# Seven products in place of eight for one unit of a weight pair, w_down in rounds, and transposes finished by gather DMAs

## The chip, the cores and the metric

One core of one Trainium2 chip runs the kernel. The metric is the device time of one execution in microseconds (us). It is set by the core's five engines, which run their own instruction queues and wait for each other through semaphores: TensorE (PE; PEld for its weight loads), VectorE (DVE), ScalarE (ACT), GpSimd (POOL) and SyncE (SP), and by 16 DMA engines.

## The reference

Two layers of a decoder trunk, batch 1, 256 positions, width 2048, all in float32. What is computed in one layer:

```python
h = rms_norm(x, mix_norm[l])
proj = h @ w_in[l]                                  # 2048 x 7680
q, k, v, uv, gate_logits = split(proj)              # 1024, 256, 256, 2048, 4096 columns
q, k = rope(rms_norm(q)), rope(rms_norm(k))         # heads of 64
branch_a = sliding_window_attention(q, k, v, sinks) @ w_attn_branch[l]      # 1024 x 2048
branch_b = chunked_sgu(gelu(uv), w_spatial, ...) @ w_sgu_branch[l]          # 1024 x 2048
merged = sigmoid(gates_a) * branch_a + sigmoid(gates_b) * branch_b
x = x + merged @ w_out[l]                           # 2048 x 2048
h2 = rms_norm(x, ffn_norm[l])
x = x + (silu(h2 @ w_gate[l]) * (h2 @ w_up[l])) @ w_down[l]   # 2048 x 5632, twice; 5632 x 2048
```

The weights, 475 MB in all, are read once from HBM.

## The kernel before, in words

**Matmuls.** A float32 product is made of three passes in the type float32r: an operand is split into a rounded part (hi) and a remainder (lo), and `a_hi w_hi + a_hi w_lo + a_lo w_hi` is summed in PSUM (lines 202, 203 and 204). One matmul takes 128 rows of the contraction, 128 positions and 512 columns.

**Chunks, parts and units.** The weights form one list of chunks of 512 columns in the order of use. A chunk is loaded in halves of 256 rows, 512 KB each, on SP's queue (`Stream.load`, L115), into one of 4 buffers `raw`. `Stream.split` makes `hi` (ScalarE, L128) and `lo` (VectorE, L129) of a half, into one of 3 buffers each; such a split half is called a part here. A part feeds 12 matmuls: 2 halves of the positions, 2 blocks of 128 rows, 3 passes. `Stream.next` keeps loads 5 and splits 3 parts ahead of the part that TensorE takes, so far as buffers are free.

The activations are held in units of 512 features, transposed (features on partitions), as `uh` and `ul`. `product(units)` runs over all parts of a chunk and sums into two PSUM banks, one for each half of the positions; four banks in all, so two chunks alternate.

**Transposes.** `transposed` turns an activation of 256 x 512. `turn` does it on VectorE, 16 instructions of 32 x 256 for each unit (L216), in four steps, and the split of the turned unit follows 4 and 5 steps after the call. With `on_pe` the turning is done by 8 TensorE transposes into two PSUM banks instead (L246); this is used for the first norm's four units and for the last unit before a product needs it. `kT` and `qT` of the attention are made by `turn` as well.

**Order.** TensorE's instructions run in the order in which the program is written. The order on the other engines is set by a scheduler that plays the program through. `after(n, fn)` puts a piece of side work (attention, gelu, transposes, norms) n slots later; `tick()` ends a slot, one for each part, and issues what is due behind the last split.

**Stages of a layer.** k/v, two chunks of q, two of v, two of u, four of the first gate, four of `w_attn_branch`, then alternately a second gate chunk and a chunk of `w_sgu_branch`, four of `w_out`, eleven times gate and up, four of `w_down` (each over all 11 hidden units). `residual` adds a finished chunk to `xs`, and prepares the next norm: its unit (2 slots later), its squares and, at the last chunk, its `rstd`.

**Slots of SBUF.** Units, gates, hidden chunks and attention tiles share one pool of 29 slots of 4 KB per partition.

Of the kernel before, what the change touches and what calls it, by code (L numbers as in the profile page):

```python
# [31 lines left out]
W_LOAD = 5  # L32
W_SPLIT = 3
N_WARM = 8
TT = 1
K_TURN = 7
Q_TURN = 7
Q_FIRST = 12
Q_STEP = 5
LOAD_BY = (1, 3, 4, 4)  # L40
# [5 lines left out]
def hybrid_trunk(ctx: ExitStack, tc: tile.TileContext, x, mix_norm, w_in, q_norm, k_norm, sinks,  # L46
# [6 lines left out]
    big = ctx.enter_context(tc.tile_pool(name="big", bufs=29))  # L53
    wraw = ctx.enter_context(tc.tile_pool(name="wraw", bufs=4))
    wsp = ctx.enter_context(tc.tile_pool(name="wsp", bufs=3))
    tmp = ctx.enter_context(tc.tile_pool(name="tmp", bufs=5))
    turned = ctx.enter_context(tc.tile_pool(name="turned", bufs=TT))
    small = ctx.enter_context(tc.tile_pool(name="small", bufs=4))
    ps_acc = ctx.enter_context(tc.tile_pool(name="ps_acc", bufs=4, space=bass.MemoryType.PSUM))
# [19 lines left out]
    def cols_of(w_ap, n):  # L79
        return [w_ap[:, j * CW:(j + 1) * CW] for j in range(n)]  # L80

    O_KV, O_U, O_V, O_GATE = QW, QW + 2 * KVW, QW + 2 * KVW + SW, QW + 2 * KVW + 2 * SW
    NF = FF // CW
    chunks = []
    for l in range(DEPTH):
        wl = w_in[l]
        for o in (O_KV, 0, CW, O_V, O_V + CW, O_U, O_U + CW):
            chunks.append(wl[:, o:o + CW])
        chunks += cols_of(wl[:, O_GATE:O_GATE + D], NCH)
        chunks += cols_of(w_attn_branch[l], NCH)  # L90
        for j in range(NCH):
            chunks.append(wl[:, O_GATE + D + j * CW:O_GATE + D + (j + 1) * CW])
            chunks.append(w_sgu_branch[l, :, j * CW:(j + 1) * CW])
        chunks += cols_of(w_out[l], NCH)
        for f in range(NF):
            chunks.append(w_gate[l, :, f * CW:(f + 1) * CW])
            chunks.append(w_up[l, :, f * CW:(f + 1) * CW])
        chunks += cols_of(w_down[l], NCH)
    halves = [(w, h) for w in chunks for h in range(w.shape[0] // (2 * P))]

    class Stream:


# [5 lines left out]
        def load(self, upto):  # L109
            while len(self.raws) < min(upto, len(halves)):  # L110
                w, h = halves[len(self.raws)]
                raw = wraw.tile([P, 2, CW], F32, tag="raw", name=nm("raw"))
                src = w[2 * h * P:2 * (h + 1) * P, :].rearrange("(k p) n -> p k n", p=P)
                if self.raws:
                    self.loaded = nc.sync.dma_start(raw, src)  # L115
                else:
                    for i in range(2):
                        self.loaded = nc.sync.dma_start(raw[:, i:i + 1], src[:, i:i + 1])
                self.raws.append(raw)

        def split(self, upto):
            while len(self.parts) < min(upto, len(halves)):
                raw = self.raws[len(self.parts)]
# [3 lines left out]
                for i in ([slice(0, 1), slice(1, 2)] if one else [slice(0, 2)]):  # L127
                    nc.scalar.activation(hi[:, i, :], raw[:, i, :], AF.Copy)  # L128
                    self.last = nc.vector.tensor_tensor(out=lo[:, i, :], in0=raw[:, i, :], in1=hi[:, i, :].bitcast(F32),  # L129
                                            op=ALU.subtract)  # L130
                self.parts.append((hi, lo))

        def next(self):
            self.load(self.at + W_LOAD)
            self.split(self.at + W_SPLIT)
            self.at += 1
            return self.parts[self.at - 1]
# [10 lines left out]
    def tick():  # L148
        slot_no[0] += 1
# [39 lines left out]
    def product(units):  # L189

        ps = [ps_acc.tile([P, CW], F32, tag="acc", name=nm("acc")) for _ in range(NT)]
        n = 2 * len(units)
        for h in range(n):
            hi, lo = stream.next()
            uh, ul = units[h // 2]
            for t in range(NT):
                for kk in range(2):
                    k = 2 * (h % 2) + kk
                    a, b = uh[:, k, t * P:(t + 1) * P], ul[:, k, t * P:(t + 1) * P]
                    first = h == 0 and kk == 0  # L200
                    last = h == n - 1 and kk == 1
                    nc.tensor.matmul(ps[t], a, hi[:, kk, :], start=first, stop=False)  # L202
                    nc.tensor.matmul(ps[t], a, lo[:, kk, :], start=False, stop=False)  # L203
                    nc.tensor.matmul(ps[t], b, hi[:, kk, :], start=False, stop=last)  # L204
            if h < n - 1:
                tick()
        return ps

    def turn(dst, src):

        iv = src.rearrange("p t (k j c) -> p t k j c", j=4, c=B)
        ov = dst.rearrange("p k (t i c) -> p t k i c", t=NT, c=B)

        def blocks(j):
            for i in range(4):
                nc.vector.transpose(ov[j * B:(j + 1) * B, :, :, i, :], iv[i * B:(i + 1) * B, :, :, j, :])  # L216

        blocks(0)
        for j in range(1, 4):
            after(j, lambda j=j: blocks(j))  # L220

    def transposed(units, c, src, scale=None, cols=None, on_pe=False):

        uh = slot([P, 4, S], F32R, "uh")
        ul = slot([P, 4, S], F32R, "ul")

        def parts(k0, n, src_t):
            step = n if cols is None else 1
            for k in range(0, n, step):
                g = (scale or 1.0) if cols is None else cols[:, k0 + k:k0 + k + 1]  # L230
                nc.scalar.activation(uh[:, k0 + k:k0 + k + step, :], src_t[:, k:k + step, :], AF.Copy, scale=g)  # L231
            for k in range(0, n, step):
                g = (scale or 1.0) if cols is None else cols[:, k0 + k:k0 + k + 1]
                kk = slice(k0 + k, k0 + k + step)
                nc.vector.scalar_tensor_tensor(  # L235
                    out=ul[:, kk, :].rearrange("p k s -> p (k s)"),
                    in0=src_t[:, k:k + step, :].rearrange("p k s -> p (k s)"), scalar=g,
                    in1=uh[:, kk, :].bitcast(F32).rearrange("p k s -> p (k s)"), op0=ALU.mult, op1=ALU.subtract)

        if on_pe:  # L240
            for b in range(2):
# [5 lines left out]
                parts(2 * b, 2, pt)  # L247
            units[c] = (uh, ul)
# [4 lines left out]
        def done():  # L253
            parts(2, 2, tt[:, 2:4])
            units[c] = (uh, ul)

        turn(tt, src)
        after(4, lambda: parts(0, 2, tt))
        after(5, done)

    class Norm:
# [13 lines left out]
        def unit(self, c, on_pe=False):  # L275
            transposed(self.units, c, xs[:, :, c * CW:(c + 1) * CW], cols=self.cols[:, 4 * c:4 * c + 4],
                       on_pe=on_pe)
# [61 lines left out]
    class Layer:  # L339


        def __init__(self, l):
# [7 lines left out]
            self.lng = lay.tile([P, SW], F32, tag="lng", name=f"lng{l}")  # L350
            self.lnb = lay.tile([P, SW], F32, tag="lnb", name=f"lnb{l}")

        def fetch(self, i, eng):
# [7 lines left out]
            else:  # L361
                dst, row = ((self.lng, sgu_ln_g), (self.lnb, sgu_ln_b))[i - 2]
                eng.dma_start(dst, row[l].unsqueeze(0).to_broadcast([P, SW]))

# [23 lines left out]
        def spatial(self):  # L388
            self.wsT = lay.tile([P, G, P], F32, tag="wsT", name=f"wsT{self.l}")
# [8 lines left out]
    def prepare(l):  # L398
        layer[l] = pl = Layer(l)
        after(6, pl.tables)  # L400
        if l:
            for i in range(4):
                pl.fetch(i, nc.gpsimd)
            after(13, pl.spatial)
            return
# [4 lines left out]
    class Attention:  # L410
# [46 lines left out]
        def keys(self, kv):  # L457
# [4 lines left out]
            after(K_TURN, lambda: turn(self.kT, kd.rearrange("p t n a d -> p t (n a d)")))  # L462

        def queries(self, c, q):
# [3 lines left out]
            after(Q_TURN, lambda: turn(self.qT[c], q))  # L468
            n = Q_FIRST + (4 * Q_STEP - 8) * c
# [4 lines left out]
            after(n + 6, lambda: transposed(self.attT, c, self.att[c]))  # L474
# [121 lines left out]
    def gate(units):  # L596
        ps = product(units)
        dst = slot([P, NT, CW], name="gate")
        for t in range(NT):
            nc.scalar.activation(dst[:, t, :], ps[t], AF.Tanh, scale=norm.rh[t])  # L600
        tick()
        return dst

    def residual(units, cols):

        nxt = Norm(cols) if cols is not None else None
        for j in range(NCH):
            ps = product(units)
            for t in range(NT):
                n = 1 if cols is not None or j < NCH - 1 else 2  # L610
                w = CW // n
                for i in range(n):
                    sl = slice(j * CW + i * w, j * CW + (i + 1) * w)
                    nc.vector.tensor_tensor(out=xs[:, t, sl], in0=ps[t][:, i * w:(i + 1) * w], in1=xs[:, t, sl],
                                            op=ALU.add)
                    if cols is None:
# [112 lines left out]
```

## Time and profile before

| | |
|---|---|
| time, median of 2 runs | 2535.38 us (2535.35 to 2535.41) |
| span of the profiled execution, first to last instruction | 2534.6 us; the runs' times are 0.8 us longer than this span |
| granted TensorE clock | 0.999 |
| TensorE, VectorE, ScalarE, GpSimd busy | 2518.1, 1772.1, 1149.8, 47.9 us |
| read from HBM | 475.27 MB, 188 GB/s over the span |

The profile is of one execution. Its parts are the busy time of each engine, 40 slices of the span, the DMA queues, the chain of work that ended last (followed back from the last instruction to what released it), the costliest groups of instructions, and the DMA issues. A group's row reads: line, engine, operation, out<-in, count | busy us, mean ns of one | idle time of the engine just before them, and what ended it. A row of the waits reads: who waited <- for whom: us in total, times, longest. A row of a stretch reads: from:to, its length, then for each engine its busy time and (xinstructions), the granted clock, the DMA share and GB/s. A row of the timeline reads: start, us, engine, line, operation, xcount. Matmuls are pipelined, so a matmul's busy time is longer than the distance to the next.

### The profile page before, as it was taken

How to read it: one execution, taken by the hardware profiler on the slowest of the kernel's cores; microseconds unless marked ns; L12 is line 12 of the kernel's file. 1: busy time of each engine (PE TensorE's matmuls, PEld its weight loads, DVE VectorE, ACT ScalarE, POOL GpSimd, SP SyncE). 2: the span in 40 equal slices, each digit the busy share in tenths (PEclk: the TensorE clock that was granted, in tenths of full speed). 3: DMA queues.
4: the chain of work that ended last, by engine and by line, in shares of the span. 5: the costliest groups of instructions: out<-in, count | busy, mean ns of one | idle time of the engine just before them, and what ended most of it. 6: DMA issues, size and time to landing. Idle time of an engine off the chain costs nothing.

```text
span 2534.6 us, 30238 instructions
## 1 busy us (share of the span) xinstructions
PE 2518.1 (99%) x11306; PEld 2079.3 (82%) x11306; DVE 1772.1 (70%) x2467; ACT 1149.8 (45%) x1386; POOL 47.9 (2%) x51
## 2 busy tenths in 40 slices
PE   9999999999999999999999999999999999999999
PEld 7788888888888888888887888888888888888887
DVE  7987767786766767665679976677767676765444
ACT  5455444454444444444444544444544444444333
POOL 1100000000000000000001000000000000000000
PEclk9999999999999999999999999999999999999999
DMA  7555666566666666666665556666666666666665
GB/s 237 175 170 147 189 198 192 191 202 196 188 195 192 193 197 191 194 195 192 193 183 165 160 151 197 191 192 197 192 191 192 197 189 196 191 198 191 203 204 158
DMA packets 248643, 479.35 MB, mean 189 GB/s; under 512 B 14960, under 2 KB 16592, under 8 KB 248496
## 3 DMA queue, kind: packets, MB, share of 16 engines
q1 hardware_dynamic: 247376, 475.33, 63.0%
q0 software_dynamic: 800, 1.83, 0.4%
q8 instruction: 88, 1.44, 0.3%
q14 instruction: 59, 0.48, 0.1%
q10 hardware_dynamic: 320, 0.27, 0.0%
HBM read 475.27 MB, written 2.10 MB: 188 GB/s over the span
## 4 chain that ended last, share of the span: by engine, by line
PE 94%; DVE 4%; issue 1%; POOL 1%; DMA 0%; ACT 0%; SPq 0%; DVEq 0%; ACTq 0%
PE acc L202 31%; PE acc L203 30%; PE acc L204 30%; DVE wlo L129 1%; DVE qT L216 1%; PE po L523 1%; POOL rq L187 1%; PE ppt L513 0%; PE psc L485 0%; DMA raw<-in_w_in_dram 0%; PE psg L587 0%; DVE kT L216 0%; PE pt L246 0%; DVE sq L441 0%; DVE q L452 0%
## 5 line engine op out<-in xcount | busy, mean ns | idle before, releaser
L129 DVE TENSOR_TENSOR wlo<-raw,whi 128x1024 fp32r<-128x1024 f32 (+1 forms) x898 | 1096.8, 1222 | 704.8 <-ACT whi L128 698.9
L128 ACT ACTIVATE whi<-raw 128x1024 fp32r<-128x1024 f32 (+1 forms) x898 | 949.3, 1058 | 1227.8 <-PE acc L204 1158.4
L203 PE MATMUL acc<-wlo,uh 128*128 128x512 f32 x3584 | 1396.8, 390 | 7.8 <-DVE wlo L129 7.7
L202 PE MATMUL acc<-whi,uh 128*128 128x512 f32 x3584 | 1400.0, 391 | 1.1 <-ACT uh L231 1.1
L204 PE MATMUL acc<-whi,ul 128*128 128x512 f32 x3584 | 1395.6, 389 | 0.0
L203 PEld LDWEIGHTS acc<-wlo,uh 128*128 128x128 f32 x3584 | 673.2, 188 | 151.6 <-DVE wlo L129 13.3
L202 PEld LDWEIGHTS acc<-whi,uh 128*128 128x128 f32 x3584 | 673.3, 188 | 140.7 <-ACT uh L231 1.9
L204 PEld LDWEIGHTS acc<-whi,ul 128*128 128x128 f32 x3584 | 673.1, 188 | 140.5 <-DVE ul L235 0.5
L216 DVE STREAM_TRANSPOSE tt<-hid 32x256 f32<-32x256 f32 x352 | 153.4, 436 | 5.7
L231 ACT ACTIVATE uh<-tt 128x512 fp32r<-128x512 f32 x72 | 41.5, 624 | 53.0 <-DVE tt L216 53.0
L216 DVE STREAM_TRANSPOSE tt<-xs 32x256 f32<-32x256 f32 x144 | 62.8, 436 | 2.3
L235 DVE SCALAR_TENSOR_TENSOR ul<-tt,uh 128x512 fp32r<-128x512 f32 x72 | 49.1, 684 | 0.0
L216 DVE STREAM_TRANSPOSE tt<-gate 32x256 f32<-32x256 f32 x96 | 41.8, 436 | 1.6
L682 ACT ACTIVATE hid<-acc,rhalf 128x512 f32<-128x512 f32 x44 | 30.4, 690 | 21.3 <-PE acc L204 21.3
L683 DVE SCALAR_TENSOR_TENSOR hid<-hid,acc 128x512 f32<-128x512 f32 x44 | 30.1, 684 | 11.6 <-ACT hid L682 11.6
L687 DVE SCALAR_TENSOR_TENSOR hid<-acc,rr,hid 128x512 f32<-128x512 f32 x44 | 30.9, 743 | 0.0
L501 ACT ACTIVATE pr<-pr,negm 128x128 f32<-128x128 f32 (+1 forms) x64 | 28.3, 443 | 5.4 <-DVE negm L494 5.3
L216 DVE STREAM_TRANSPOSE tt<-att 32x256 f32<-32x256 f32 x64 | 27.9, 436 | 1.1
L216 DVE STREAM_TRANSPOSE tt<-u 32x256 f32<-32x256 f32 x64 | 27.9, 436 | 1.0
L216 DVE STREAM_TRANSPOSE qT<-q 32x256 f32<-32x256 f32 x64 | 27.9, 436 | 0.9
L600 ACT ACTIVATE gate<-acc,rhalf 128x512 f32<-128x512 f32 x32 | 22.0, 689 | 13.5 <-PE acc L204 13.5
L187 POOL TENSOR_TENSOR rstd<-var,neg_half 128x1 f32<-128x1 f32 x8 | 5.2, 662 | 1142.5 <-DVE var L284 1142.4
(110 smaller groups left out, 573.3 us busy)
## 6 DMA issues: line engine op xcount, KB each, us to landing
raw<-in_w_in_dram SPq DMA_DIRECT2D x239, 512.0 KB, 4.0
raw<-in_w_gate_dram SPq DMA_DIRECT2D x176, 512.0 KB, 3.8
raw<-in_w_up_dram SPq DMA_DIRECT2D x176, 512.0 KB, 3.9
raw<-in_w_down_dram SPq DMA_DIRECT2D x176, 512.0 KB, 4.2
raw<-in_w_out_dram SPq DMA_DIRECT2D x64, 512.0 KB, 3.8
raw<-in_w_attn_branch_dram SPq DMA_DIRECT2D x32, 512.0 KB, 4.2
raw<-in_w_sgu_branch_dram SPq DMA_DIRECT2D x32, 512.0 KB, 4.1
xs<-in_x_dram SPq DMA_DIRECT2D x8, 256.0 KB, 7.7
```

What stands on the lines that cost most here:

```text
L128: nc.scalar.activation(hi[:, i, :], raw[:, i, :], AF.Copy)
L129: self.last = nc.vector.tensor_tensor(out=lo[:, i, :], in0=raw[:, i, :], in1=hi[:, i, :].bitcast(F32), op=ALU.subtract)
L187: nc.gpsimd.tensor_tensor(out=dst, in0=src, in1=neg_half[:, :n], op=ALU.pow)
L202: nc.tensor.matmul(ps[t], a, hi[:, kk, :], start=first, stop=False)
L203: nc.tensor.matmul(ps[t], a, lo[:, kk, :], start=False, stop=False)
L204: nc.tensor.matmul(ps[t], b, hi[:, kk, :], start=False, stop=last)
L216: nc.vector.transpose(ov[j * B:(j + 1) * B, :, :, i, :], iv[i * B:(i + 1) * B, :, :, j, :])
L231: nc.scalar.activation(uh[:, k0 + k:k0 + k + step, :], src_t[:, k:k + step, :], AF.Copy, scale=g)
L235: nc.vector.scalar_tensor_tensor(out=ul[:, kk, :].rearrange("p k s -> p (k s)"), in0=src_t[:, k:k + step, :].rearrange("p k s -> p (k s)") ...
L682: nc.scalar.activation(th, ps[t], AF.Tanh, scale=norm.rh[t])
L683: nc.vector.scalar_tensor_tensor(out=th, in0=th, scalar=1.0, in1=ps[t], op0=ALU.add, op1=ALU.mult)
L687: nc.vector.scalar_tensor_tensor(out=a[:, t, :], in0=ps[t], scalar=norm.rr[t], in1=a[:, t, :], op0=ALU.mult, op1=ALU.mult)
```

## The change

- **Pairs and loads.** Chunks are taken in pairs of 1024 columns (k/v alone stays 512 wide; the last gate and up chunk form one pair). A load is 1 MB: 256 rows of a pair. Four `raw` buffers of this size, five split buffers (3 before). The parts stay 256 rows x 512 columns.
- **`run(units, done)`** takes the place of `product`. A pair sums into all four accumulator banks; `done(c, ps)` reads column half c as soon as it is finished.
- **Seven products.** For one unit of each pair in `w_out`, gate/up and `w_down` (`M_OUT`, `M_FFN`, `M_DOWN` = 1) the block of 256 positions x 512 rows x 1024 columns is cut into 2 x 2 x 2 and computed by Strassen's method in the form that needs 4 differences of weights, 4 sums of activations and 7 block products. `Stream.split` makes the differences in place in `raw` on VectorE; `combined` makes the sums for the unit. Between the products ScalarE copies four times out of PSUM (two of these copies go to another bank) and VectorE adds twice into a bank. A slot of side work is two such products long.
- **w_down in rounds.** The hidden chunks come in rounds of 4, 4 and 3; after each the residual of this round is added to `xs`.
- **Transposes.** `gathered` takes the place of `turn`: two VectorE instructions transpose the 32 x 32 blocks of a unit in place, and 16 DMAs on GpSimd's queue, 32 KB each, bring the blocks to their places. The reader follows `G_WAIT` = 8 slots after. The turning on TensorE is used for more units: the last two of each residual, of the merged and of each round's hidden units, and one of the attention's.
- **Others.** 23 slots of 4 KB in place of 29; the SGU's scale, shift and `wsT` lie in slots; scores start at slot 19 (12 before).

The core of the diff:

```diff
-W_LOAD = 5
-W_SPLIT = 3
+W_LOAD = 4
+W_SPLIT = 5
+ROUNDS = ((0, 1, 2, 3), (4, 5, 6, 7), (8, 9, 10))
+M_OUT, M_FFN, M_DOWN = 1, 1, 1
...
+    PRODUCTS = ("11", "t1", "t2", "22", "t3", "21", "t4")
...
+                src, total = {"11": ("11", None), "22": ("22", None), "21": ("21", None),
+                              "t1": ("11", ("12", "11")), "t2": ("11", ("22", "11")),
+                              "t3": ("12", ("22", "12")), "t4": ("11", ("21", "11"))}[name]
...
+                raw = self.raws[i][j]
+                if total is not None:
+                    (ia, ja), (ib, jb) = total
+                    nc.vector.tensor_tensor(out=raw, in0=self.raws[ia][ja], in1=self.raws[ib][jb], op=ALU.subtract)
...
+        own = [acc(b) for b in (banks if job.pair else banks[:2])]
+        if job.m:
+            a, e, x, y = own
+            ps = [[x, y], [e, a]]
+            banks[:] = [banks[2], banks[3], banks[1], banks[0]]
+            into = {"11": a, "t1": e, "t2": a, "22": e, "t3": a, "21": x, "t4": y}
...
+            if name != "whole":
+                p = into[name]
+                for k in range(2):
+                    ah, al = unit.block(name, k)
+                    three(p, ah, al, hi[:, k, :], lo[:, k, :], id(p) not in begun, at and k == 1)
+                    begun.add(id(p))
+                if at:
+                    with tc.high_priority():
+                        if name == "11":
+                            nc.scalar.activation(x, a, AF.Copy)
+                        elif name == "t1":
+                            kept("p5", e)
+                        elif name == "t2":
+                            kept("u2", a)
+                        elif name == "22":
+                            nc.vector.tensor_tensor(out=e, in0=e, in1=held["u2"], op=ALU.add)
+                        elif name == "t3":
+                            nc.scalar.activation(y, a, AF.Copy)
+                            nc.vector.tensor_tensor(out=a, in0=a, in1=held["p5"], op=ALU.add)
+                if n < len(job.steps) - 1:
+                    tick(0.5)
+                continue
...
+    def gathered(dst, src):
+
+        blk = turned.tile([P, 4, 4, NT, B], F32, tag="blk", name=nm("blk"))
+        for t in range(NT):
+            nc.vector.transpose(blk[:, :, :, t, :].rearrange("p j k c -> p k j c"),
+                                src[:, t, :].rearrange("p (k j c) -> p k j c", j=4, c=B))
+        ov = dst.rearrange("p k (t i c) -> p i (k t) c", t=NT, c=B)
+        for i in range(4):
+            for j in range(4):
+                nc.gpsimd.dma_start(ov[j * B:(j + 1) * B, i],
+                                    blk[i * B:(i + 1) * B, j].rearrange("p k t c -> p (k t) c"))
...
+        def combined(f):
+            s4 = slot([P, 4, 2, P], name="sums")
+            a11, a12, a21, a22 = (f[:, 2 * h:2 * h + 2, t * P:(t + 1) * P] for t in range(2) for h in range(2))
+            for i, (p, q, op) in enumerate(((a21, a22, ALU.add), (s4[:, 0], a11, ALU.subtract),
+                                            (a11, a21, ALU.subtract), (a12, s4[:, 1], ALU.subtract))):
+                nc.vector.tensor_tensor(out=s4[:, i], in0=p, in1=q, op=op)
+            two(unit.hi, unit.lo, f)
+            two(unit.shi, unit.slo, s4)
+            units[c] = unit
...
+        gathered(tt, src)
+        after(G_WAIT, done)
...
+                if nxt is not None:
+                    after(2, lambda: nxt.unit(o, on_pe=j == 2, sums=sums and o == 0))
...
+                after(2, lambda: transposed(hT, f, a, on_pe=f in fs[-2:], sums=f in fs[:M_DOWN]))
```

More of the change, by code (lines that the diff above doesn't have):

```diff
@@ L196, in product @@
             for t in range(NT):
+                p = ps[c][t]
                 for kk in range(2):
[L198 to L220, printed above, removed]
@@ L240, in transposed @@
         if on_pe:
+            f = turned.tile([P, 4, S], F32, tag="tt", name=nm("tt")) if sums else None
             for b in range(2):
```

441 lines of the change are left out of this document (281 added, 160 removed).

## The prediction

> **What bounds the kernel now.** I read the shares of the engines and the chain first, then the groups of instructions that write or read the accumulators, then a stretch of TensorE's timeline for the pitch, then the waits.
>
> ```profile
> span 2534.6 us, 30238 instructions
> PE 2518.1 (99%) x11306; PEld 2079.3 (82%) x11306; DVE 1772.1 (70%) x2467; ACT 1149.8 (45%) x1386; POOL 47.9 (2%) x51
> q1 hardware_dynamic: 247376, 475.33, 63.0%
> PE 94%; DVE 4%; issue 1%; POOL 1%; DMA 0%; ACT 0%; SPq 0%; DVEq 0%; ACTq 0%
> 0.00:2535.00 2535.00, 2457.17 (x10752) 2014.94 (x10752) 123.27 (x182) 63.32 (x92) 1.00 0.64 189
> ```
>
> The last row is the stretch of the whole run for instructions on the accumulators (busy time of PE, PEld, DVE, ACT): 10752 of TensorE's 11306 matmuls are products with a weight. TensorE carries 94% of the chain; VectorE has 30% free and the DMA queue a third. A matmul's busy time overlaps its neighbours', so its price is the pitch:
>
> ```profile
> 899.65 0.39 PE L202 MATMUL acc<-whi,uh 128*128 128x512 f32 x1
> ...
> 909.85 0.39 PE L202 MATMUL acc<-whi,uh 128*128 128x512 f32 x1
> ```
>
> 45 matmuls lie between these starts: 10.20 / 45 = 0.2267 us. 10752 of them make 2437 us of the span of 2534.6; head, tail, attention and waits share the other 97. So time is gained by issuing fewer matmuls, and lost by letting TensorE wait. It hardly waits now:
>
> ```profile
> SPq L115 <- DVE wlo L129: 1967.7, 843, 6.8
> ACT whi L128 <- PE acc L204: 1158.4, 708, 3.4
> DVE wlo L129 <- ACT whi L128: 698.9, 602, 3.1
> PEld acc L203 <- DVE wlo L129: 13.3, 14, 1.9
> PE acc L203 <- DVE wlo L129: 7.7, 12, 1.5
> ACT whi L128 <- DMA raw<-in_w_in_dram: 3.4, 2, 2.8
> ```
>
> Loads wait for the split, the split for TensorE; only 7.7 us go the other way. Weights are not short, and bigger loads buy nothing by themselves.
>
> **Part 1: the matmuls that go.** A unit (512 rows of the contraction, 1024 columns of a pair) costs 4 parts x 12 = 48 matmuls; by seven products of 2 x 3 = 6 it costs 42. One unit per pair is done so: 2 pairs in w_out, 4 + 4 + 3 in gate/up, 2 x 3 in w_down, 19 per layer, 38 in all. 38 x 6 = 228 matmuls x 0.2267 = **51.7 us** off TensorE. The operands keep tile shape and type, so I keep the pitch.
>
> **Part 2: the transposes that come to TensorE.** Units turned there rise from 9 (72 transposes) to 28: merged 4, attention 2, norms 4 at the start, 4 + 2 at the residuals, hidden 12. One such unit stands in the trace:
>
> ```profile
> 1814.38 0.39 PE L204 MATMUL acc<-whi,ul 128*128 128x512 f32 x1
> 1814.62 1.04 PE L246 MATMUL pt<-ident,xs 128*128 128x128 f32 x8
> 1815.41 0.48 PE L202 MATMUL acc<-whi,uh 128*128 128x512 f32 x1
> 1815.72 0.40 PE L203 MATMUL acc<-wlo,uh 128*128 128x512 f32 x1
> ...
> 1815.83 1.55 ACT L231 ACTIVATE uh<-pt,vcols 128x256 fp32r<-128x256 f32 x4
> ...
> 1817.10 1.65 DVE L235 SCALAR_TENSOR_TENSOR ul<-pt,vcols,uh 128x256 fp32r<-128x256 f32 x4
> ```
>
> From 1814.38 to 1815.72 is 1.34 us where two pitches take 0.45: 0.89 a unit, 19 x 0.89 = **+16.9**. Nine times two such units follow within 2.7 us on the same two PSUM buffers, and the second waits until both engines have read the first. Nothing in the trace shows that pair. Its cost lies between 0 and the 2.92 us (1815.83 to 1818.75) for which a unit is read; since the second comes up to 2.7 us later, I take 0.5 each, near the lower end: **+4** (0 to 26).
>
> **Part 3: what the seven products ask of VectorE and ScalarE.** The rows:
>
> ```profile
> L129 DVE TENSOR_TENSOR wlo<-raw,whi 128x1024 fp32r<-128x1024 f32 x894 | 1094.2, 1224 | 702.1 <-ACT whi L128 696.3
> L128 ACT ACTIVATE whi<-raw 128x1024 fp32r<-128x1024 f32 x894 | 946.8, 1060 | 1227.2 <-PE acc L204 1158.4 <-ACT whi L128 26.4 <-issue 25.9
> L614 DVE TENSOR_TENSOR xs<-acc,xs 128x512 f32<-128x512 f32 x30 | 19.2, 682 | 0.0
> L614 DVE TENSOR_TENSOR xs<-acc,xs 128x256 f32<-128x256 f32 x4 | 1.5, 419 | 5.1 <-PE acc L204 5.1
> L600 ACT ACTIVATE gate<-acc,rhalf 128x512 f32<-128x512 f32 x32 | 22.0, 689 | 13.5 <-PE acc L204 13.5
> 0.00:2535.00 2535.00, 355.61 (x816) 1.00 0.64 189
> ```
>
> (The last is the whole run for the transposes of L216.) Per unit: 7 splits in place of 4 and 4 differences of weights at 1.22, so +8.5 us on VectorE, and +3.2 on ScalarE; 2 sums at 0.68 on VectorE and 4 copies at 0.69 on ScalarE. Over 38 units that is +377 on VectorE and +226 on ScalarE. Three rounds of w_down bring 32 more residual sums (+22), ten units with sums about 2.8 each (four sums of 256 elements at 0.42, 1.22 for one more split, less 0.1), +28. The transposes fall from 356 us to 64 x 0.68 = 44 (estimate from the 512-element row). VectorE 1772 + 377 + 22 + 28 - 312 = **1887 us**, about three quarters of the span: as a mean it fits beside TensorE and costs nothing. In the stretch of seven products it may not. TensorE needs 42 x 0.2267 = 9.5 us for them. Five split buffers mean that four parts are ready when the first product starts; VectorE still owes, within those 9.5 us, 2.44 (t3), 1.22 (21), 2.44 (t4), 1.22 (the first whole part), 1.36 (two sums) and 1.36 (the previous pair's output): 10.04, so 0.5 too much; nothing, if one difference was taken early. Above lies a chain in which VectorE, at one of the differences, idles through ScalarE's 1.06 because the next step needs it: 0.5 + 1.06, about 1.6. I take 0.3, nearest to the sum of rows: 38 x 0.3 = **+11** (0 to 61). A copy out of PSUM adds a wait on TensorE (product t2 writes the bank that ScalarE copies, t3 and t4 likewise), with one product, 1.36 us, to cover 0.17 of drain and 0.69 of copy. What is queued behind on ScalarE are splits of 1.06; one of them ahead of the copy costs 0.5, counted in the upper end.
>
> **Part 4: transposes by gather DMAs.** 32 groups of 16 issues on GpSimd's queue, 32 KB each in runs of 128 B. The nearest rows are two loads of the same size and the same runs:
>
> ```profile
> 1.60 0.89 POOL L313 DMA_DIRECT2D cs<-in_cosine_dram  x1
> 2.50 0.73 POOL L314 DMA_DIRECT2D sn<-in_sine_dram  x1
> 3.22 0.54 POOL L319 DMA_DIRECT2D vrows<-in_mix_norm_dram  x1
> cs<-in_cosine_dram POOLq DMA_DIRECT2D x1, 32.0 KB, 4.5
> sn<-in_sine_dram POOLq DMA_DIRECT2D x1, 32.0 KB, 5.2
> ```
>
> Issues follow each other at 0.73 to 0.89 without waiting for a landing. Sixteen at 0.75 are 12 us, the last lands 4.5 later: 16.5. The reader stands 8 slots of 2.72 us (a part of 12 matmuls) behind: 21.8. So one gather is covered. The added wait stands on ScalarE, with later parts' splits behind it, and TensorE's four parts, 10.9 us, behind those. The block and target tiles have one buffer each: of two units gathered in a row, the second's issues wait until the first is read (about 26 us after the first began), so it is ready at 26 + 16.5 + 3 = 46. On GpSimd's queue the norms' powers stand behind at most 12 us of issues: q and k are issued 7 slots (19 us) after their pair, the next powers come with the next pair, 43.5 us on. Merged, hidden and attention units have over 60 us. The residual's have not: after w_out the next pair (42.2 us) and the Strassen unit (9.5) cover it; after layer 0's w_down the last round's pair is 31.3 and the next unit is wanted 5.4 + 1.8 later, at 38.5: TensorE waits **+7** there (0 if issues run at 0.54; 15 if at 0.89 and late).
>
> The Trainium skill speaks against this: "DMA: Bandwidth & Descriptors", Anatomy of one DMA, fits a GpSimd DMA as 2.0 us plus bytes over 436 GB/s, by which 16 in a row would be 33 us, past the 21.8, an estimate from that page. The trace disagrees as to the order: the rows above show such DMAs overlapped, so the sum keeps 16.5.
>
> **Part 5: the rest.** 1 MB loads: four buffers still, twice the bytes each, and SP waits 1968 us for buffers; nothing, and up to 4 us in the head if that cover were gone. Four accumulator banks for a pair leave an output 2.7 us to be read, against 0.68 + 0.69 of work: nothing, up to 1 us in each of 4 gelu jobs. The first stage of each layer may gain:
>
> ```profile
> 60.00:125.00 65.00, 61.05 (x279) 47.78 (x277) 61.56 (x94) 30.26 (x46) 9.02 (x4) 1.00 0.56 166
> 1310.00:1380.00 70.00, 66.41 (x302) 52.91 (x301) 65.08 (x100) 29.69 (x37) 7.62 (x2) 1.00 0.55 160
> ```
>
> VectorE is full there (61.56 of 65) and TensorE idles 3.95 and 3.59. Turning q and k leaves VectorE with about 17 us less a layer; I take **-5** of those 7.5 (0 to -10).
>
> **Sum.** 2534.6 - 51.7 + 16.9 = 2499.8 for TensorE's own work; + 4 + 11 + 7 - 5 = 2516.8, and 0.8 us lie outside the span (the runs' median is 2535.38). **2517 us**, 0.7% under before. All waits at nothing and the full gain at the layers' heads: 2490.
>
> **Rivals.**
> *All edits hidden.* For it: 30% free on VectorE. Against: 10.04 us owed in 9.5. 2490 to 2500.
> *VectorE takes the saving back:* seven products last as long as eight did, 10.9 instead of 9.5. For it: 13.4 us of splits and differences per unit against 9.5 of matmuls, with PE-turned units' reads on top after w_out and up. 38 x 1.36 = 51.7 on 2506: about 2558. That is also the case in which the change does not do what it says.
> *The queues block (slower):* ScalarE's queue has the read of the second gathered unit where its slot puts it, 24.5 us after the first began, and it lands at about 43: 18 us, of which 10.9 are covered, 7 to 8 us at nine such pairs (2 merged, 3 residual, 4 hidden), 65 us: 2590. It decides from a pair that ends later than 35 us, and grows with the issue time: at 0.89 each pair costs 3 to 5 more. Its extreme, sixteen DMAs one behind another at the landing time of 4.5, is 72 us a gather and 39 past all cover, over 1200 us in 32 of them; issues 0.9 apart with landings of 4.5 speak against that, and I give it 0.01 of the 0.15 below. The skill's fit, named above, lies between the two. Against it: the order on ScalarE and VectorE isn't written out by hand, only TensorE's is, so a late read may stand later. "SBUF — State Buffer", Door 1, adds that VectorE's two-port copies can starve GpSimd's descriptors; no run here shows it, and most of VectorE's work here has two inputs.
>
> **Chances.** 2% of 2535 (2485, 2586) is about what a measurement of this kernel can tell from no change. Forecast (2500 to 2540) 0.50; all hidden 0.20; saving taken back 0.15; queues block 0.15. Faster by over 2% needs 2485, below every sum here: 0.02, out of the second. Slower: the last case less a tenth of it, 0.13. Within: 0.85. The range 2490 to 2570 leaves out the blocked queues and little else.
>
> **What would show it.** 10524 matmuls on the accumulators, 224 transposes into pt, 1010 splits, 152 differences, 512 issues of 32 KB on GpSimd's queue; VectorE near 1887 us busy. TensorE's waits on wlo inside the seven products near 0.3 us a unit; one wait of several us for uh at the start of layer 1. Wrong if the pitch moves, if an issue from SBUF to SBUF takes over 1.3 us (sixteen then pass 21.8), if ScalarE shows long waits for gather DMAs, or if TensorE waits for copies out of PSUM.

## The result: slower, because TensorE waits and then runs at half clock

The changed kernel takes **2641.72 us** (2641.45 to 2641.99) against 2535.38: a ratio of 1.0421, 95% interval 1.0391 to 1.0451. Forecast were 2517 and 2490 to 2570. The page of after: span, engines, the chain, the groups that the change adds, the gathers' landing:

```profile
span 2640.2 us, 29935 instructions
PE 2527.0 (96%) x11230; PEld 2075.9 (79%) x11230; DVE 1844.4 (70%) x2125; ACT 1335.3 (51%) x1658; POOL 338.3 (13%) x559
...
PE 86%; DVE 8%; ACT 3%; issue 2%; DMA 1%; POOL 0%; SPq 0%; DVEq 0%; ACTq 0%
...
L189 DVE TENSOR_TENSOR raw<-raw,raw 128x1024 f32<-128x1024 f32 x114 | 139.1, 1220 | 2.6
L189 DVE TENSOR_TENSOR raw<-raw 128x1024 f32<-128x1024 f32 x38 | 46.6, 1226 | 1.3
L358 POOL DMA_DIRECT2D tt<-blk x416 | 239.4, 583 | 1911.8 <-DVE blk L353 1236.6
...
tt<-blk POOLq DMA_DIRECT2D x416, 32.0 KB, 4.0
```

Its view of cores (span and granted clock), and the whole run as one stretch for the accumulators' instructions (busy time of PE, PEld, DVE and ACT; clock, DMA share, GB/s):

```profile
core 0: 2640.2 us, clock 0.981
```
```profile
0.00:2642.00 2642.00, 2446.89 (x10524) 1992.41 (x10524) 199.03 (x290) 150.14 (x244) 0.98 0.57 188
```

The work is as counted beforehand: 10524 matmuls on the accumulators and 152 differences. The gathers issue in 0.58 us and land in 4.0 (median). But TensorE's part of the chain fell from 94 to 86%, and the clock from 0.999 to 0.981. TensorE's waits in after (engine, waiting group, whom for: us in total, times, longest):

```profile
PE pt L400 <- DVE ul L375: 28.8, 9, 7.5
PE acc L262 <- ACT sq L710: 17.9, 7, 4.8
PE acc L262 <- DVE hid L861: 17.1, 4, 4.3
PE acc L262 <- ACT acc L303: 12.7, 6, 2.1
PE po L692 <- DVE pr L657: 7.8, 8, 2.4
...
PE acc L262 <- ACT gate L822: 5.5, 2, 2.8
...
PE acc L263 <- DVE wlo L195: 0.8, 1, 0.8
```

None of the long ones is for a weight (last row). The whole view has 109.5 us, where before had 12.7. All but some 12 of the 109.5 are waits for a bank or a PSUM buffer that ScalarE or VectorE has not read yet; the rest are for other things, such as the source of a transpose. ScalarE itself hardly waits for gathers to land (its one row of this kind):

```profile
ACT uh L371 <- DMA tt<-blk: 2.8, 1, 2.8
```

The stretch in which the forecast saw TensorE idle for 3.95 us before has no idle time in after (columns PE, PEld, DVE, ACT, POOL, clock, DMA share, GB/s):

```profile
60.00:125.00 65.00, 65.00 (x292) 53.95 (x291) 43.76 (x44) 26.78 (x26) 25.11 (x36) 1.00 0.70 224
```

I sort the distances between starts of neighbouring matmuls: **own work** is every pair at its usual distance, **waits** the excess where TensorE stood idle over 0.1 us, **slow clock** the excess inside the trace's intervals of half clock. For four of the kernels, in us (a row's four parts do not add up to the time: 6 to 9 us lie before the first matmul, behind the last and outside the profiled execution):

```
                     time     own work  waits  slow clock  rest of the excess
before               2535.4   2500.1     13.3      1.7       14.4
after                2641.7   2467.7    106.8     40.5       19.9
mended (below)       2512.6   2467.0     14.2      2.0       20.7
mended, no seven     2556.9   2518.8     10.1      1.8       19.1
```

The change saved 32.4 us of work and lost 93.5 in waits, 38.8 in clock, 5.5 in the rest: +105. Which distance counts as usual is a choice: another fair one moves up to 9 us between own work and the rest, but their sum falls by 26.9 either way, and waits and slow clock stay within 0.5 us.

**One wait in full.** The timeline of after at the first matmul of an up pair (start, duration; idle time before it and its releaser in brackets):

```profile
712.37 5.17 POOL L358 DMA_DIRECT2D tt<-blk  x9 [15.54 <-DVE sums L388]
...
718.76 3.46 POOL L358 DMA_DIRECT2D tt<-blk  x6 [1.22 <-DMA tt<-blk]
...
723.29 0.39 PE L264 MATMUL acc<-whi,ul 128*128 128x512 f32 x1
723.78 1.06 ACT L194 ACTIVATE whi<-raw 128x1024 fp32r<-128x1024 f32 x1 [1.42 <-PE acc L264]
724.74 1.13 ACT L371 ACTIVATE uh<-tt 128x512 fp32r<-128x512 f32 x2
725.78 2.40 ACT L860 ACTIVATE hid<-acc,rhalf 128x512 f32<-128x512 f32 x4
727.21 2.47 DVE L861 SCALAR_TENSOR_TENSOR hid<-hid,acc 128x512 f32<-128x512 f32 x4
727.95 0.50 PE L262 MATMUL acc<-whi,uh 128*128 128x512 f32 x1 [4.27 <-DVE hid L861]
...
728.98 0.62 PE L263 MATMUL acc<-wlo,uh 128*128 128x512 f32 x1
729.40 0.63 PE L264 MATMUL acc<-whi,ul 128*128 128x512 f32 x1
```

Two stretches of it, before the wait and after (columns as above, with POOL's busy time behind ACT's):

```profile
716.00:724.00 8.00, 7.68 (x34) 6.01 (x33) 6.72 (x7) 3.30 (x4) 5.57 (x10) 1.00 0.45 140
728.90:732.40 3.50, 3.50 (x11) 2.71 (x10) 1.54 (x3) 1.54 (x2) 0.00 (x0) 0.51 0.00 0
```

The second gathered unit may go out only when the first is read out of the one tile `tt` (712.37). Its issues end at 722.2; its read stands at 724.74 in ScalarE's queue *ahead* of the four activations that empty the gate pair's accumulators, which TensorE wants next. VectorE's are later still, and TensorE idles 4.27 us. The read does not wait for its landing: ScalarE works without a break from 723.78 on. Ahead of it stands a split that had waited 1.42 us for TensorE, and everything behind is late by that as well. A microsecond after TensorE starts again, the clock is at half for 3.4 us (last row: 11 matmuls, clock 0.51; starts 0.42 apart instead of 0.23).

The waits on line 303 are another case, four banks with no gathered read ahead (the timeline again):

```profile
636.96 1.28 DVE L861 SCALAR_TENSOR_TENSOR hid<-hid,acc 128x512 f32<-128x512 f32 x2
...
638.07 0.60 ACT L289 ACTIVATE p<-acc 128x512 f32<-128x512 f32 x1
638.57 1.05 ACT L194 ACTIVATE whi<-raw 128x1024 fp32r<-128x1024 f32 x1
639.51 0.59 ACT L303 ACTIVATE acc<-acc 128x512 f32<-128x512 f32 x1
640.15 0.75 PE L262 MATMUL acc<-whi,sh 128*128 128x512 f32 x1 [2.12 <-ACT acc L303]
```

Product 11 must be copied into a bank of the previous pair, which VectorE reads until 638.24; then a split of 1.05 us goes first, and t2, which needs the bank that is copied, waits.

### The profile page after: what moved, and what is told of

Its sections match the earlier page's. It is cut to its first block, busy times and chain, and to the rows that moved or that the text cites. A ratio compares the mean times of both kernels' runs of the same rounds, so it can differ in the third digit from the quotient of the medians.

```text
span 2640.2 us, 29935 instructions
## 1 busy us (share of the span) xinstructions
PE 2527.0 (96%) x11230; PEld 2075.9 (79%) x11230; DVE 1844.4 (70%) x2125; ACT 1335.3 (51%) x1658; POOL 338.3 (13%) x559
## 4 chain that ended last, share of the span: by engine, by line
PE 86%; DVE 8%; ACT 3%; issue 2%; DMA 1%; POOL 0%; SPq 0%; DVEq 0%; ACTq 0%
PE acc L262 28%; PE acc L264 28%; PE acc L263 28%; DVE wlo L195 3%; ACT whi L194 2%; DVE raw L189 1%; PE po L692 1%; PE pt L400 1%; DVE ul L375 1%; DVE hid L866 0%; ACT junk L441 0%; PE psc L654 0%; PE ppt L682 0%; DVE blk L353 0%; DMA xs<-in_x_dram 0%
## 5 line engine op out<-in xcount | busy, mean ns | idle before, releaser
L195 DVE TENSOR_TENSOR wlo<-raw,whi 128x1024 fp32r<-128x1024 f32 (+1 forms) x1012 | 1220.5, 1220 | 689.1 <-ACT whi L194 688.1
L194 ACT ACTIVATE whi<-raw 128x1024 fp32r<-128x1024 f32 (+1 forms) x1012 | 1058.1, 1057 | 1124.2 <-PE acc L264 877.0
L262 PE MATMUL acc<-whi,uh 128*128 128x512 f32 x3204 | 1261.5, 394 | 44.9 <-ACT sq L710 17.9
L264 PE MATMUL acc<-whi,ul 128*128 128x512 f32 x3204 | 1254.0, 391 | 3.0 <-DVE ul L375 2.9
L263 PE MATMUL acc<-wlo,uh 128*128 128x512 f32 x3204 | 1253.6, 391 | 0.8 <-DVE wlo L195 0.8
L358 POOL DMA_DIRECT2D tt<-blk x416 | 239.4, 583 | 1911.8 <-DVE blk L353 1236.6
L262 PE MATMUL acc<-whi,sh 128*128 128x512 f32 x304 | 127.6, 420 | 14.8 <-ACT acc L303 12.7
L189 DVE TENSOR_TENSOR raw<-raw,raw 128x1024 f32<-128x1024 f32 x114 | 139.1, 1220 | 2.6
L263 PE MATMUL acc<-wlo,sh 128*128 128x512 f32 x304 | 124.5, 409 | 0.0
L264 PE MATMUL acc<-whi,sl 128*128 128x512 f32 x304 | 123.7, 407 | 0.0
L358 POOL DMA_DIRECT2D qT<-blk x64 | 36.9, 584 | 58.4 <-DVE blk L353 40.0
```

Of the source, the lines that this page charges most:

```text
L189: nc.vector.tensor_tensor(out=raw, in0=self.raws[ia][ja], in1=self.raws[ib][jb], op=ALU.subtract)
L194: nc.scalar.activation(hi[:, k, :], raw[:, k, :], AF.Copy)
L195: self.last = nc.vector.tensor_tensor(out=lo[:, k, :], in0=raw[:, k, :], in1=hi[:, k, :].bitcast(F32), op=ALU.subtract)
L262: nc.tensor.matmul(ps, a, hi, start=first, stop=False, skip_group_check=True)
L263: nc.tensor.matmul(ps, a, lo, start=False, stop=False, skip_group_check=True)
L264: nc.tensor.matmul(ps, b, hi, start=False, stop=last, skip_group_check=True)
```

## The experiments

Two theories at first. ORDER: TensorE waits because the reads of PSUM stand late in ScalarE's and VectorE's queues. LOAD: VectorE has too much to do in the seven products (the forecast's own rival). Later ORDER was parted into BANKS and QUEUE (gathered units).

**What a pause costs.** The kernel before, with 22 pauses added: a small matmul waits for a power on GpSimd.

```
+ nc.scalar.activation(seen[:, :n], ps[:, :n], AF.Square); rsqrt(slow[:, :n], seen[:, :n], n)
+ nc.tensor.matmul(pz[:, :n], ident, slow[:, :n], start=True, stop=True)
  # e4: n = 16 (layer 0), 4 (layer 1);  e13: n = 6, 7, 8, 9, 10, 12 mixed
```

> The kernel before with 22 pauses: after each gate product TensorE waits for a ScalarE copy of 16 columns, a power on GpSimd (16 columns, about 3.8 us, in layer 0; 4 columns, about 1.25 us, in layer 1) and one small matmul. Measures what a wait of TensorE costs beyond its own length. If only the wait counts: 11 x about 5.2 and 11 x about 2.6 us, 2620 us, and the granted clock stays at 0.999. If each wait brings a stretch of 3.4 us at half clock behind it (1.7 us each, twice as much after the longer ones): 2655 to 2680 us, granted clock about 0.98.

> The kernel before with 22 pauses of TensorE again, their lengths now mixed: a power on GpSimd over 6 to 12 columns (by the two lengths of the earlier run about 1.7, 1.9, 2.0, 2.2, 2.35 and 2.7 us idle). EDGE (idle time alone decides, near 2 us, since 11 pauses of 1.4 cost no clock, 10 of 11 of 3.3 did, and waits of 2.1 in the changed kernel did): no half clock after 6 or 7 columns, half clock after most of 9 to 12. PHASE (the clock is judged in windows of 3.4 us, so what counts is how a pause lies in one): about the same length sometimes falls and sometimes not, more often the longer it is, with 8 to 10 mixed. Time: 2534 + 22 x 2.3 + about 25 for the clock: about 2600.

Measured 2620.24 and 2623.07. In e4 the pauses of layer 1 were 1.4 us, shorter than I had planned, so its time alone would have looked like "waits only"; the trace parts it: 51.7 us of waits, 23.6 of slow clock, the rest the added matmuls. Of the 11 pauses of 3.3 us, 10 were followed or accompanied by half clock, of the 11 of 1.4 us none. From e13, stretches behind the pauses of 1.68, 1.83 and 2.04 us, and around one of 2.68:

```profile
577.00:580.40 3.40, 3.40 (x16) 2.83 (x17) 1.23 (x1) 0.14 (x2) 0.00 (x0) 1.00 0.53 163
623.96:627.38 3.42, 3.42 (x10) 2.65 (x9) 0.09 (x1) 0.00 (x0) 0.00 (x0) 0.50 0.56 177
671.75:675.16 3.41, 3.41 (x10) 2.73 (x10) 0.80 (x1) 0.00 (x0) 0.00 (x0) 0.50 0.59 181
815.11:821.94 6.83, 6.26 (x16) 5.00 (x17) 0.95 (x1) 0.30 (x1) 0.52 (x1) 0.50 0.35 112
```

Where the clock is halved, a stretch of 3.41 us has 10 matmuls instead of 16 (those that only touch it counted too). Of 7 pauses of 1.68 to 1.89 us, 3 cost it, of 15 from 2.04 to 2.68, 14. (e13's time lies above the 2600 expected.)

PHASE is the one that holds. In each trace the stretches of half clock begin on one grid of 3.413 us. Cut the twenty traces of this case into these windows, leave out the first 30 us, and take those at full clock: of those in which TensorE stood idle for 1.95 us or more, 150 of 150 were followed by a window at half clock; from 1.4 to 1.95 us, 19 of 102; below 1.4 us, 4 of 14481. So the idle time inside one window counts, not the length of one wait. Of the six waits of 2.12 us on line 303 of after, the four that lay in one window were followed by half clock; the two that fell across an edge were not. Nor were its two waits of 2.76 us (0.84 and 1.92 in one case). A window at half clock costs about 1.4 us (six matmuls fewer at 0.2267; in after 40.5 us in some 30 such windows).

**Parts undone one at a time in the changed kernel.** e1: eight products for eight, `M_OUT, M_FFN, M_DOWN = 0, 0, 0`. e2: no gathered units, `if on_pe:` becomes `if True:`. e3: `hid` gets a pool of its own, so that its reads are put ahead of those of gathered units. e9: VectorE turns blocks in place of the gathers, as before the change.

> The changed kernel with no seven products (M_OUT, M_FFN, M_DOWN = 0), everything else kept. TensorE gets back 228 x 0.2267 = 51.7 us of matmuls. Theory LOAD (VectorE, with 11 passes of 1.22 us in the 9.5 us of seven products, reads the accumulators late): TensorE's waits and the halved clock fall to about those of before (13 + 2 us in place of 107 + 40): about 2560 us. Theory ORDER (reads of PSUM stand on ScalarE and VectorE behind the split of a gathered unit that is not there yet, because tiles of one pool get their buffers in program order): only the six waits for the copy out of PSUM go, 14 us and their slow clock: about 2670 us, 2655 to 2690.

> The changed kernel with all 26 gathered units turned on TensorE (only kT and the two qT are still gathered). TensorE gets 26 x 0.89 = 23 us more. ORDER: the waits behind gathered units go (hidden chunks 4 x 4.4, residual 2 x 6.8, layer boundary 7.6, gates 2 x 2.9, together 45 us, and about 17 us of halved clock): about 2603 us. LOAD: the waits stay: about 2665 us.

> The changed kernel with the hidden chunks in a pool of their own (2 buffers; 21 slots left for the rest, so the same memory). No instruction is added or taken; only the order on ScalarE and VectorE can change. ORDER: the four waits of 4.4 us at the second up pair of rounds 1 and 2 go, 17.7 us, and some 8 us of halved clock behind them: about 2616 us. LOAD: within 0.3% of 2642 us.

> Only the gathers are undone: where the changed kernel gathers, VectorE turns blocks of 32 as before the change (16 instructions, three slots), the reader four slots behind, attention's slots as before. QUEUE (reads of gathered units stand ahead of the accumulators' reads on ScalarE and VectorE): waits on hid (17.1), on pt at 592 and 1335 (21) and on gate (5.5) go, with some 20 us of half clock; the waits on sq and on the copies stay: about 2590. VECTOR (VectorE, at 1844 us, gets some 150 us more and is late in the seven products): 2640 or more, with waits on wlo or ul.

Measured 2628.45, 2628.22, 2631.85 and 2662.67. The first three lie between their theories. In e1 the copies' waits go, but those on hid (12.0) and sq (18.0) stay: in the changed kernel the seven products cost 13 us net. TensorE's waits in e2, e3 and e9, two rows each:

```profile
PE acc L262 <- ACT acc L303: 21.2, 10, 2.1
PE acc L262 <- ACT sq L710: 17.9, 7, 4.8
```
```profile
PE pt L401 <- DVE ul L376: 31.1, 9, 9.8
PE acc L263 <- ACT acc L304: 21.5, 10, 2.2
```
```profile
PE acc L263 <- DVE wlo L195: 36.8, 28, 2.9
PE acc L262 <- ACT acc L303: 21.5, 10, 2.2
```

In e2 the waits on hid and gate are gone and pt's fall to 8.7, but where hid had been late the copy of line 303 now is (10 waits instead of 6). e3 shows the same, and the layer boundary gets worse: what one read gains, the next loses. e9 is the first with real waits for weights: without gathers VectorE is busy 2025 us, and VECTOR, which is LOAD under another name, comes true. QUEUE's signs come too (the waits on hid and gate are gone, pt's fall to 14.0), but the time goes to weights and copies. Against VectorE's blocks the gathers are worth 21 us.

**Banks.** e5: six accumulator banks from the second gates on (the two of the attention products are free then). e6: q, v and u by single chunks, two banks each. e7: e1 and e2 together, so that pairs, rounds, 1 MB loads and the gathers of the attention's kT and qT are left.

```
e5  + if b > 3: return ps_at.tile([P, CW], F32, tag=f"at{b - 4}", name=nm("acc"))
    + banks[:] = [4, 5] + banks        # before the gates of gb; a job takes banks[:4]
e6  - for o in (0, O_V, O_U, ...): add_job([wl[:, o:o + CW2]])
    + for o in (0, CW, O_V, O_V + CW, O_U, O_U + CW): add_job([wl[:, o:o + CW]])
```

> From the gates of the second branch on, a pair takes its four accumulators from six banks (the two of the attention products are free by then), so a new job's first two banks have been idle for a whole pair. BANKS (four banks leave a read 2.7 us, and ScalarE or VectorE often comes later): the waits of TensorE on hid (17.1), on the copy of line 303 (12.7), on gate (5.5) go, 35 us, and with them about 17 of the 40 us at half clock: about 2588. ORDER (the engines read late in any case, and what is late is late for the next bank too): over 2630.

> q, v and u are taken one chunk of 512 columns at a time, two banks each, as before the change; all else as in the changed kernel. BANKS: the waits on line 710 (17.9 us) fall to under 4 and some 8 us of half clock go with them: about 2617. LOAD (VectorE is full in that stage and gives the time back elsewhere): 2635 or more, with waits on wlo in place of those on sq.

> No seven products and no gathered units: every unit is turned by TensorE, and pairs, rounds of w_down and 1 MB loads are all that is left of the change. TensorE's own work 2490 + 52 = 2542. BANKS: the pairs alone keep the waits on sq (17.9), some on hid and gate (15) and their half clock (about 15): about 2600. Rival (seven products and gathers make the waits): 2560.

Measured 2633.17, 2635.25, 2631.86. BANKS alone fell. In e5 the copy is late for another reason, the gathered read and the reads of hid ahead of it:

```profile
PE pt L409 <- DVE ul L384: 32.0, 9, 10.7
PE acc L269 <- ACT acc L312: 21.9, 4, 5.5
```

In e6 the waits on sq go as BANKS said, but a good part comes back in attention's small products, and the clock stays at 0.981. Its time is the one that LOAD gave, but by luck: LOAD's sign, waits on wlo, is not there (0.8 us). e7 missed both forecasts, 2600 and 2560: pairs alone keep 16.9 us on sq and 20 us of slow clock, and attention waits longer than before; it has 45 more units turned by TensorE than before, own work 2548.7.

**All together.** e8 joins six banks, chunks, all units on TensorE, and half of the first load behind x's second block. e12 is e8 without seven products. e11 takes over e8's banks, chunks and load and keeps gathers, but one per group (`on_pe=o > 0` and likewise), splits three parts ahead instead of five at the head, and turns the last two units of a group three slots behind their output instead of two. e10 is e11 with VectorE's blocks in place of gathers, on the units that the change gathers, and attention's slots as before. e14 is e11 with the second unit of every pair four slots behind its output, and attention's scores and values one slot later; its expectation speaks of every unit, but the first of a pair stays where e11 has it.

> Six banks, q, v and u by chunks, all units turned by TensorE, and the second half of the first load behind the second block of x. Seven products, pairs, rounds and 1 MB loads stay. If the four causes are the whole loss: TensorE's own work 2490, waits near 25, others 20, half clock under 10: about 2540, the time of the kernel before. If the order of reads stays late whatever the banks: 2590 or more.

> The kernel of the run named all_mended (2589.3) with eight products for eight: no seven products, nothing else changed. If the seven products keep their saving once the banks are mended: TensorE's own work 2495 + 53, waits 45 - 10: 2632. If their chain of copies and sums gives it back: about 2605 or less.

> The same with six banks from the second gates on, q, v and u by chunks, three splits instead of five ahead at the head, and the last two units of each group turned one slot later. If the named causes are all: TensorE's own work 2468, waits near 25, others 21, half clock 8, ends 7: about 2529. If VectorE is the bound then: over 2560, with waits on wlo.

> Gathers are kept for the first unit of each group alone, the other units turned by TensorE; six banks, chunks, head and slots as in the run named six_chunks. TensorE's own work 2478. If only a second gathered unit is late (it waits for the block tile): waits near 25, half clock 8, others 21, ends 7: about 2539. If a single gathered unit is late too: 2570.

> The kernel of the run named one_gather (2552.8) with every unit that TensorE turns issued one slot later, the second of a pair two, attention's products one slot later. If its waits on pt and po (some 25 of 40 us) are sources and PSUM buffers read too late: about 2537. If they move with the slots (other reads come late then): 2550.

Measured 2589.27 (e8: what was expected if reads come late whatever the banks), 2614.15 (e12: seven products bring 25 us there, half their saving), 2598.43 (e10: VectorE is the bound, 28 waits on wlo), 2552.80 (e11) and **2512.87** (e14). One or two slots (2.7 us each) more for sources and PSUM buffers were worth 40 us, where I had expected 15: waits fell from 40.0 to 15.6, slow clock from 6.7 to 1.7, and own work and rest together by 11 (a wait that nearly every pair of a kind has counts as own work).

**One cause at a time put back into the mended kernel.** e15 is e14 again, for its interval; e16 has four banks, e17 two gathered units in a row, e18 no seven products.

```
e16  - banks[:] = [4, 5] + banks
e17  - on_pe=j + c > 0    + on_pe=j == 2        (likewise residual, hid)
e18  - M_OUT, M_FFN, M_DOWN = 1, 1, 1    + 0, 0, 0
```

> The kernel of the run named one_gather_later again, in five rounds against the kernel before: 2512.9, a ratio near 0.991 with an interval below 1.

> The same with four accumulator banks throughout, as the change has them. BANKS: the waits on the copy into the next pair's bank (2.3 us each, 6 to 10 of them) and on hid or gate come back with half clock behind them: 2513 + 15 + 10 = about 2538. If the later slots alone had mended it: about 2515.

> The same as the mended kernel with two gathered units in a row again, as the change has them (TensorE's own work 10 us less). QUEUE: the reads of the second gathered unit stand ahead of the accumulators' and PSUM's reads on ScalarE and VectorE, waits of 5 to 10 us at pt and acc come back, 55 us in all, with 25 of half clock: about 2580. If six banks and slots cover them: 2503.

> The mended kernel with eight products for eight. If the seven products keep their whole saving there (228 matmuls at 0.2267): 2513 + 52 - 4 (their copies' waits) = about 2560. If they give a good part back: 2540 or less.

Measured: e15 **2512.63**, ratio 0.9911 to before, interval 0.9898 to 0.9925; e16 2547.30 (+34.7); e17 2570.96 (+58.3); e18 2556.93 (+44.3). The engines in e15's page, and TensorE's longest waits of e16 and e17:

```profile
PE 2489.4 (99%) x11302; PEld 2057.0 (82%) x11302; DVE 1827.4 (73%) x2107; ACT 1324.8 (53%) x1658; POOL 258.7 (10%) x415
```
```profile
PE acc L271 <- ACT acc L312: 21.2, 10, 2.1
```
```profile
PE acc L278 <- ACT acc L321: 21.9, 4, 5.5
PE pt L418 <- DVE rhalf L475: 13.9, 2, 6.9
PE acc L278 <- ACT uh L389: 6.2, 2, 4.9
```

Four banks bring back ten waits of 2.1 us on the copy, and half clock behind six of them (14.4 us of slow clock); two gathered units the long waits on the copy, on pt and at the layer boundary (slow clock 20.3). With neither, no wait is over 1.5 us and e15's clock stays at 0.999. In e17 too ScalarE waits for a landing only once, 3.2 us, so the place of the reads does it and not the gathers' speed. These two causes are shown. Chunks for q, v and u, the slots and the changed head were not put back one at a time in this kernel; e6 and e11 against e14 are all there is on them. The shares are not to be added to the 105 us, since e2, e3 and e5 showed that what one mending frees the other cause takes.

## Why the prediction was wrong, step by step

- **Part 1 was right.** In the mended kernel eight for eight costs 2518.8 - 2467.0 = 51.8 us more own work (51.7 forecast) and 44.3 of time.
- **Part 2** was about right in TensorE's own work: with part 1 it forecast -34.8, measured -32.4 (-26.9 with the rest). Pairs of PE-turned units on two PSUM buffers, taken at +4 in a range to 26, are under-sized: e11 still waited 8.2 us at pt for reads and 12 for sources; one to two slots of distance removed it.
- **Part 3** was right on VectorE: it is busy 1844 us (1887 forecast), and waits for weights are 0.8 us. *VectorE takes the saving back* fell; it holds in e9 and e10, where VectorE has 2019 us or more. The +11 is near only by luck: the seven products' own loss is 51.8 - 44.3 = 7.5 us in the mended kernel, but e15's waits there are for ScalarE's copies (4.6 us on `u`) and not for VectorE. The step that failed is the copy, given "one product, 1.36 us, to cover 0.17 of drain and 0.69 of copy". It left out that product 11 is copied into a bank that the previous pair's reader still holds: 2.12 us each, 12.7 in after and 21.2 in e16. "TensorE waits for copies out of PSUM" was one of the signs of being wrong.
- **Part 4 failed** at the second of two gathered units. It asked when TensorE wants the unit ("over 60 us") and saw only later splits, covered by four parts, behind a late read on ScalarE. It did not count the reads of accumulators and of pt in the same queues, which have 2.7 us. Issues took 0.58 instead of 0.75, and the second unit of the pair above had landed 38 us after the first began (46 forecast): it was not the landing but the place of the read. The rival *The queues block* named that place, but its mechanism, ScalarE waiting for the landing, shows at the layer boundary alone (2.8 us); "long waits for gather DMAs" did not come. That it gave 65 us of waits and e17 is 58 us longer is luck: e17 has 49 us more waits, 18 more of slow clock and 7 less own work. The forecast's +7 at the boundary is near the wait of 7.5 us there, but TensorE waits for pt, whose reads stand behind the gathered unit's. What the prediction cites from the Trainium skill's page "SBUF — State Buffer" stands there in the section "SBUF: two separate sides", not in Door 1.
- **Part 5 failed**: "four accumulator banks ... nothing, up to 1 us in each of 4 gelu jobs" is 34.7 us in the mended kernel, and 17.9 of waits on sq alone in after. It set 2.7 us against the work of the reads, and left out what stands before them in the queues. The "-5" came where it was expected: in the stretch 60 to 125 TensorE is busy throughout, and layer 1 has no idle time in this stage either, up to the waits on sq. But the start of the kernel lost more, and the forecast put nothing there: five splits ahead of the second unit's read put the 96th matmul on the accumulators at 41.5 us instead of 34.7 (41.1 in e8, which has half of the first load later; 36.9 in e11, which has three splits ahead as well).
- **Missing altogether:** that a wait can cost more than its length. 40.5 us of the loss are slow clock. Before had only waits up to 1.5 us and one stretch of half clock, so its trace gave no price. The Trainium skill names the effect: "TensorE: Matmul & The Clock Gate", Part 1, says that the clock is halved after an idle window of about 3.4 us and that windows run free. The traces agree on the window (3.41 us), but a window that was idle for 1.95 us was already enough, in all 150 cases here.
- The sum itself, 2516.8, lies near the 2512.6 of the mended kernel, and part of that is luck: this kernel turns nine more units on TensorE (8 us by part 2's price) and has no wait at the layer boundary.

Open stays the rest of the excess (19.9 against 14.4), in after and mended alike.

## What to carry to other kernels

When a kernel hands a buffer over with one step of slack, ask for each engine what stands in its queue between the write and the read; a mean share of 73% says nothing about it. Price each wait by its length, and where some 2 us of idle time can fall into one window of 3.4 us, by about 1.4 us on top. When a large change gains nothing, mend several handovers at once: undone singly, each mending only moved the wait to the next reader, and the mended whole was then taken apart by putting one cause back at a time.

## What the runs showed of the hardware

Half clock is granted by windows of 3.413 us on one grid. A window in which TensorE stood idle for 1.95 us or more was followed by one at half clock in 150 of 150 cases, from 1.4 to 1.95 us in 19 of 102. By single pauses: 3 of 7 of 1.68 to 1.89 us and 14 of 15 of 2.04 to 2.68, two windows after 2.68; it can begin before the wait has ended (815.11 for a pause that ended at 815.68). GpSimd's gathers of 32 KB from SBUF to SBUF issue every 0.58 us and land in 4.0, overlapped.
